# The second layer's up projection as seven block products on a fused two-layer kernel

## The chip, the cores and the metric

The kernel runs on one core of one Trainium2 chip as a single program. The metric is the device time of an execution in microseconds. The core has a matrix engine (PE, with its weight loads shown apart as PEld), a vector engine (DVE), an activation engine (ACT), Pool (GpSimd), and SP, whose queue issues the transfers here. Operands lie in SBUF; matmuls write PSUM, where the kernel has three tiles `mm` of 1024 fp32 values per partition and two tiles `ms` of 512.

## The reference

Two layers over 512 tokens of width 1024, with a context of 256 tokens in the first. The first layer's mixer is a Fourier and long-convolution block, the second's an attention with low-rank queries and keys. Behind each mixer stands the same feed-forward network, and the change lies in the second layer's:

```python
def _conv_ffn(h, w_up, conv_w, conv_b, w_down):
    gate, val = jnp.split(h @ w_up, 2, axis=-1)
    return (jax.nn.silu(_dwconv3(gate, conv_w, conv_b)) * val) @ w_down
...
        x = x + g1 * yx
        x = x + g2 * _conv_ffn(_modulate(_rms_norm(x, norm2[i]), sh2, sc2), *ffn)
```

`w_up` is 1024 x 5632 (a gate half and a value half of 2816 each), `_dwconv3` mixes three neighbouring tokens of a feature, `w_down` is 2816 x 1024. All is fp32.

## The kernel before

Every fp32 product is made of three matmuls in the rounded format fp32r. A tensor is split in a high part, which ACT rounds (`hi`, line 98), and a low part, the rest, which DVE subtracts (`lo`, line 103). `mm3` (lines 123 to 125) multiplies high by high, weights' high by tokens' low, and weights' low by tokens' high. Weights stand still in PE and tokens stream through; tokens lie transposed, features on the partitions, so a tile `hh[k]` / `hl[k]` holds 128 features of all 512 tokens.

Weights come through the pool `W`, which has three buffers each of `wr` (as loaded, by SP), `wh` and `wl`. `wload` loads 128 x 1024 values and splits them. The pool gives a new tile any buffer that is free by the order of the program.

The second layer's FFN is `ffn` (line 826). Its 2816 hidden features are 22 chunks f of 128. `up(f)` loads a gate tile and a value tile of `w_up`, runs 8 x 2 x 3 matmuls of 512 columns into two PSUM tiles, then the convolution (`conv3`, lines 322 to 324: one ACT pass and two DVE taps, all reading PSUM), Silu on ACT (line 845), the product with the value half on DVE (line 847), and the split into `ah` and `al`. Chunk 0 runs as two halves of 256 tokens, since the normalization in front of it ends in halves.

The down projection runs in three groups, chunks 0 to 7, 8 to 15 and 16 to 21. Each begins when one chunk more than the group has been emitted:

```python
        for gi, (f0, f1) in enumerate(GROUPS):
            while nxt < min(f1 + 1, NF):
                up(nxt)
                nxt += 1
```

A group is `res_proj` (line 791): eight output tiles m, each with one `w_dn` tile through `wload`, 24 matmuls of 512 columns (18 in the last group), and one DVE instruction (line 808) that adds the gated result to the residual `x[m]`. The last group does its last four m in halves of 256 tokens.

In front of the FFN stands the attention's output projection, also a `res_proj`, with the normalization's work hooked between its tiles (`norm_hook`): per feature tile and half a scaling on DVE (line 266), an ACT pass that adds the shift and rounds (267), and a DVE instruction for the low part (271).

A scheduler in the framework orders each engine's instructions from what the program emits; an engine then runs its queue strictly in that order.

Of the kernel before, what the change touches and what calls it, by code (L numbers as in the profile page):

```python
# [18 lines left out]
P = 128  # L19
D = 1024  # L20
KD = 8
T = 512
# [3 lines left out]
NF = 22  # L26
GROUPS = ((0, 8), (8, 16), (16, 22))
# [23 lines left out]
class Builder:  # L51
# [169 lines left out]
    def norm(self, i, k, x, hh, hl, c0, n, tp):  # L221


        nc = self.nc
        j = 1 if c0 >= C0 else 0
        box = {}
# [47 lines left out]
        def apply(d, step=None):  # L274
# [3 lines left out]
                ins = low(d)  # L278
            return ins

        return stat, fin, apply

    def norm_hook(self, first, second):

# [541 lines left out]
    def ffn(self, i, x, hh, hl, width, segs, first_segs, late, fill=None, hook=None, rest=None):  # L826
# [42 lines left out]
        self.close(f"ftm{i}")  # L869
        self.close(f"act{i}")  # L870

    def layer0(self):
        nc, I = self.nc, self.I
        yh, yl = self.mixer()
        nt = self.pool("nt", bufs=3)
        hp = self.pool("h2p")
        self.xp = self.pool("xres")
        tp = lambda: self.t(nt, [P, 512], F32, "nt")
        x = [self.t(self.xp, [P, TW], F32, f"xr{d}") for d in range(KD)]
# [38 lines left out]
        nhook, rest = norms(1, 0)  # L918
# [30 lines left out]
    def attention(self, x, hh, hl, rest):  # L949
        nc, I = self.nc, self.I  # L950
        v = nc.vector
        sg = ((0, 512), (512, 260))
        st = ((0, T), (C0, C))
        tok = [128 * k for k in range(4)] + [C0, C0 + 128]
        dr = self.pool("dr", space=bass.MemoryType.DRAM)
        xd = self.t(dr, [KD, P, T], F32, "xd")
# [29 lines left out]
        for a in range(2):  # L986
            r = tp()
# [213 lines left out]
        self.close("pq")  # L1201
        self.close("psB")
        self.ps = self.pool("psA", space=PSUM)
        oh, ol = [], []
        op = self.pool("op")
        for p in range(KD):
            oh.append(self.t(op, [P, T], F32R, f"oh{p}"))
            ol.append(self.t(op, [P, T], F32R, f"ol{p}"))
# [1 line left out]
            self.lo(ol[p], O[p], oh[p])  # L1210
        self.close("pO")
        self.close("pa")
        return oh, ol, xd

    def layer1(self, x, hh, hl, rest):
        nc, I = self.nc, self.I
        oh, ol, xd = self.attention(x, hh, hl, rest)
        nt = self.pool("nt", bufs=3)
        hp = self.pool("h2p")
        self.xp = self.pool("xres")  # L1220
        tp = lambda: self.t(nt, [P, 512], F32, "nt")
        x = [self.t(self.xp, [P, T], F32, f"xr{d}") for d in range(KD)]
        for d in range(KD):
            nc.sync.dma_start(x[d], xd[d])
        half = [[(0, 256)], [(256, 256)]]
        hh = [self.t(hp, [P, T], F32R, f"hh{d}") for d in range(KD)]
        hl = [self.t(hp, [P, T], F32R, f"hl{d}") for d in range(KD)]
        hook, rest = self.norm_hook(*[self.norm(1, 1, x, hh, hl, c, 256, tp) for c in (0, 256)])
        self.res_proj(1, 2, oh, ol, KD, lambda m: I["w_o"][m], x, [(0, T)], half, hook)
        rest()  # L1230
        self.dbg("xa1", x)
        self.ffn(1, x, hh, hl, T, [(0, T)], half, None)
        return x

    def build(self):
        nc = self.nc
        self.setup()
        x = self.layer1(*self.layer0())
        for d in range(KD):
            nc.sync.dma_start(self.out[d], x[d][:, 0:T])  # L1240
        for n in ("xres", "h2p", "nt", "op", "dr", "psA", "sm", "W", "P0"):
            self.close(n)


# [195 lines left out]
```

## Time and profile before

| what | value |
|---|---|
| median of 3 runs | 1831.08 us (1829.17 to 1833.47) |
| profiled execution | 1830.64 us, span 1828.8 us |
| mean granted PE clock | 0.958 |
| PE busy | 1706.3 us, 93% of the span |
| DVE busy | 1022.0 us, 56% |
| ACT busy | 613.9 us, 34% |
| Pool busy | 121.3 us, 7% |
| HBM | 94 GB/s over the span |

Lines such as L103 are lines of the kernel. A group's row tells engine, line, operation, written tile <- read tiles (buffer numbers left out), shapes and counts. A timeline row has start, duration, engine, line, operation, and in brackets how long the engine had idled and what ended that. Matmul rows are pipelined, so a matmul's cost is read from start to start and not from its duration. One part of the page gives the span in 40 slices, with the busy share in tenths and the granted PE clock, another the chain of work that ended last. The second layer's FFN lies from about 1450 us to the end.

### The profile page before, as it was taken

What the parts mean: (1) busy time and instruction counts of PE and PEld (TensorE: products, weight loads), DVE (VectorE), ACT (ScalarE), POOL (GpSimd) and SP (SyncE); (2) the same over time, 40 slices, a digit from 0 to 9 for tenths busy, and PEclk for the clock granted to TensorE, in tenths of its full rate; (3) what the DMA queues carried; (4) which work ended last, traced back from release to release, by engine and by line L of the source; (5) the groups of instructions that cost most, each with busy time, mean ns of one, the idle gap of its engine ahead of it and who ended that gap; (6) DMA issues with size and microseconds to landing.
All of it is one profiled execution on the core that took longest, in us unless ns stands there. A gap on an engine that the chain in (4) does not pass through costs nothing.

```text
span 1828.8 us, 21719 instructions
## 1 busy us (share of the span) xinstructions
PE 1706.3 (93%) x8742; PEld 1326.3 (73%) x8742; DVE 1022.0 (56%) x1662; ACT 613.9 (34%) x830; POOL 121.3 (7%) x202
## 2 busy tenths in 40 slices
PE   6889975799899999999999887899998999999999
PEld 2657864787688888888888556555554777888887
DVE  3486966864898435543434554665764554444443
ACT  3332222323323212222122434655663443223231
POOL 0052113310000000000000000110110000000000
PEclk7799987899999999999999998899999999999999
DMA  9032520352355234431312310000002323322322
GB/s 351 24 127 71 171 78 30 103 173 81 116 174 176 88 104 140 147 128 70 121 47 85 117 60 24 1 12 12 12 12 70 116 72 101 104 93 92 104 75 98
DMA packets 53249, 172.83 MB, mean 95 GB/s; under 512 B 6043, under 2 KB 8925, under 8 KB 52125
## 3 DMA queue, kind: packets, MB, share of 16 engines
q1 hardware_dynamic: 53149, 171.45, 27.4%
q8 instruction: 69, 1.13, 0.2%
q14 instruction: 31, 0.25, 0.0%
HBM read 167.23 MB, written 4.19 MB: 94 GB/s over the span
## 4 chain that ended last, share of the span: by engine, by line
PE 77%; DVE 11%; ACT 5%; POOL 3%; issue 3%; DMA 1%; POOLq 0%; SPq 0%; ACTq 0%; DVEq 0%
PE mm L123 21%; PE mm L124 20%; PE mm L125 20%; PE pv L1176 2%; PE ms L234 2%; PE z L1164 2%; DVE junk L210 2%; DVE wl L103 1%; DVE S L1154 1%; PE s L1130 1%; ACT S L1145 1%; PE s L123 1%; PE s L124 1%; PE s L125 1%; POOL s L388 1%
## 5 line engine op out<-in xcount | busy, mean ns | idle before, releaser
L123 PE MATMUL mm<-hh,wh 128*128 128x512 f32 (+2 forms) x1344 | 474.7, 356 | 7.0 <-ACT wh L98 3.4
L124 PE MATMUL mm<-hl,wh 128*128 128x512 f32 (+2 forms) x1344 | 473.9, 353 | 4.9 <-DVE hl L271 4.6
L125 PE MATMUL mm<-hh,wl 128*128 128x512 f32 (+2 forms) x1344 | 473.2, 353 | 1.3 <-DVE wl L103 1.3
L98 ACT ACTIVATE wh<-wr 128x1024 fp32r<-128x1024 f32 (+2 forms) x200 | 206.2, 1031 | 717.5 <-PE mm L124 646.5
L103 DVE TENSOR_TENSOR wl<-wr,wh 128x1024 fp32r<-128x1024 f32 (+2 forms) x200 | 243.6, 1219 | 287.3 <-ACT wh L98 279.6
L123 PEld LDWEIGHTS mm<-hh,wh 128*128 128x128 f32 x1344 | 254.4, 190 | 57.1 <-issue 12.0
L124 PEld LDWEIGHTS mm<-hl,wh 128*128 128x128 f32 x1344 | 255.0, 190 | 42.9 <-DVE hl L271 7.5
L125 PEld LDWEIGHTS mm<-hh,wl 128*128 128x128 f32 x1344 | 254.5, 190 | 38.4 <-issue 2.5
L123 PE MATMUL mm<-ah,wh 128*128 128x512 f32 (+1 forms) x528 | 187.8, 356 | 0.0
L124 PE MATMUL mm<-al,wh 128*128 128x512 f32 (+1 forms) x528 | 187.7, 356 | 0.0
L125 PE MATMUL mm<-ah,wl 128*128 128x512 f32 (+1 forms) x528 | 187.3, 355 | 0.0
L210 DVE SCALAR_TENSOR_TENSOR junk<-wr,sb 128x1024 bf16<-128x1024 f32 x128 | 159.3, 1244 | 36.7 <-DMA wr<-wmodT 36.6
L808 DVE SCALAR_TENSOR_TENSOR xr<-mm,mod,xr 128x512 f32<-128x512 f32 (+1 forms) x100 | 62.2, 642 | 204.3 <-PE mm L125 204.0
L123 PEld LDWEIGHTS mm<-ah,wh 128*128 128x128 f32 x528 | 99.1, 188 | 19.2 <-DVE xr L808 2.5
L124 PEld LDWEIGHTS mm<-al,wh 128*128 128x128 f32 x528 | 99.2, 188 | 15.3 <-issue 0.8
L125 PEld LDWEIGHTS mm<-ah,wl 128*128 128x128 f32 x528 | 99.2, 188 | 14.6
L1145 ACT ACTIVATE S<-s,rks 128x512 f32<-128x512 f32 x96 | 63.4, 688 | 44.3 <-PE s L125 43.4
L1154 DVE TENSOR_TENSOR S<-S,mb 128x1536 f32<-128x1536 f32 x32 | 54.8, 1752 | 20.7 <-POOL mb L1151 20.7
L845 ACT ACTIVATE fg<-fg 128x772 f32<-128x772 f32 (+1 forms) x44 | 32.6, 741 | 100.3 <-DVE fg L324 89.3
L1176 PE MATMUL pv<-S,V 128*64 128x512 f32 x192 | 58.9, 620 | 0.0
L1164 PE MATMUL z<-S,ones 128*32 128x512 f32 x192 | 42.7, 699 | 13.7 <-ACT S L1155 11.3
L1155 ACT ACTIVATE S<-S 128x1536 f32<-128x1536 f32 x32 | 47.1, 1481 | 18.0 <-DVE S L1154 18.0
(318 smaller groups left out, 2282.6 us busy)
## 6 DMA issues: line engine op xcount, KB each, us to landing
wr<-w_up SPq DMA_DIRECT2D x88, 512.0 KB, 3.3
wr<-wmodT SPq DMA_DIRECT2D x80, 512.0 KB, 3.3
wr<-w_dn SPq DMA_DIRECT2D x32, 512.0 KB, 3.2
wm<-wmod0a SPq DMA_DIRECT2D x8, 1024.0 KB, 9.6
wr<-w_in SPq DMA_DIRECT2D x16, 512.0 KB, 3.2
wr<-w_dn SPq DMA_DIRECT2D x20, 384.0 KB, 3.1
wr<-w_out SPq DMA_DIRECT2D x12, 512.0 KB, 3.2
wr<-w_o SPq DMA_DIRECT2D x12, 512.0 KB, 3.2
```

Source lines behind the costliest of these rows:

```text
L98: self.nc.scalar.activation(dst, src, AF.Copy)
L103: (eng or self.nc.vector).tensor_tensor(dst, src, hi.bitcast(F32), op=ALU.subtract)
L123: mmul(out, wh, xh, start=start, stop=False)
L124: mmul(out, wh, xl, start=False, stop=False)
L125: mmul(out, wl, xh, start=False, stop=stop)
L210: nc.vector.scalar_tensor_tensor(junk, raw, 1.0, self.sb[:, j, :], op0=ALU.mult, op1=ALU.mult, accum_out=acc)
L808: nc.vector.scalar_tensor_tensor(x[m][:, a2:b2], ps[:, a2:b2], mod[:, 8 * sec + m, j : j + 1], x[m][:, a2:b2], op0=ALU.mult, op1=ALU.add)
L1145: nc.scalar.activation(S[j // 3][:, j % 3, :], ps, AF.Copy, scale=rs[:, 2 * j + a : 2 * j + a + 1])
L1154: v.tensor_tensor(s, s, mb3.to_broadcast([P, 3, T]), op=ALU.subtract)
L1155: nc.scalar.activation(s, s, AF.Exp)
L1164: nc.tensor.matmul(z[32 * g : 32 * g + 32, :], self.ones32, Ss[g // 2][(2 * k + g % 2) // 3][:, (2 * k + g % 2) % 3, :], start=k == 0, sto ...
L1176: nc.tensor.matmul(pv[64 * a : 64 * a + 64, :], V[:, k, 64 * h : 64 * h + 64], Ss[a][k // 3][:, k % 3, :], start=k == 0, stop=k == 5, tile ...
```

## The change

The second layer's up projection no longer multiplies whole chunks. Split the inner 1024 into two halves, the 512 tokens into two halves, and a chunk's output into gate and value: that is a 2 x 2 by 2 x 2 block product, in which eight block products of 128 x 512 by 512 x 256 are replaced by seven, in Winograd's form of Strassen's algorithm, with sums of blocks ahead and behind. Each block product is 4 x 3 matmuls of 256 columns.

- `layer1` keeps the normalized tokens as plain fp32 (`hf`, in buffers of the later `act1` pool) and as four quarter blocks in high and low parts. `apply_f` makes them: the scaling on DVE, the shift on ACT, then a separate rounding on ACT and the low part on DVE.
- `combos`, called after chunk 0, makes four sums of token blocks: 16 Pool instructions of 256 columns, each result split by ACT and DVE into `T1` to `T4`.
- Chunks 0 and 1 go the old way (`plain`), both in halves of 256 tokens.
- For chunks 2 to 21 `weights(f)` loads both `w_up` tiles, lets Pool form four sums of 512 columns in `s13` and `s24` (one buffer each), and splits four tiles: the gate tile (through `W`), half of the value tile (`vh`, `vl`, low part on Pool), `s13` (`zh`, `zl`), and `s24` (through `W`). It is emitted one chunk ahead of `strassen(f)`.
- `strassen(f)` runs the seven products into PSUM and adds them up on DVE, with two ACT copies and two Pool adds; the gate part is put together in `G` in SBUF, from where the convolution reads it, and the value part in an SBUF tile.
- The group rule stays, so `weights(9)` and `weights(17)` are emitted ahead of the down projections of the first and second group.

```diff
+    def apply_f(self, d, src, fin, f, h, l, tp):
+        n = src.shape[-1]
+        A, B = self.A[1][1][:, 0, :], self.mod[1][:, 24:32, 0]
+        u = tp()
+        self.nc.vector.scalar_tensor_tensor(u[:, :n], src, A[:, d : d + 1], fin.box["R"][:, :n], op0=ALU.mult, op1=ALU.mult)
+        self.nc.scalar.activation(f, u[:, :n], AF.Identity, bias=B[:, d : d + 1])
+        self.hi(h, f)
+        self.lo(l, f, h)
...
+    def ffn_s(self, i, x, hf, quarter, ap, nt):
...
+        zp = self.pool("zp", bufs=2)
+        tm = self.pool("ftm", bufs=2)
...
+        def combos():
+            for k in range(4):
+                a, b = hf[k], hf[k + 4]
...
+                g.tensor_tensor(t1, a[:, H:], a[:, :H], op=ALU.subtract)
+                g.tensor_tensor(t2, b[:, H:], t1, op=ALU.subtract)
+                g.tensor_tensor(t3, b[:, H:], a[:, H:], op=ALU.subtract)
+                g.tensor_tensor(t4, t2, b[:, :H], op=ALU.subtract)
+                for n, t_ in enumerate((t1, t2, t3, t4)):
+                    self.hi(tq[n + 1, 0][:, k, :], t_)
+                    self.lo(tq[n + 1, 1][:, k, :], t_, tq[n + 1, 0][:, k, :])
...
+        def weights(f):
+            a1, a2 = (self.wraw(I["w_up"][i, f, q]) for q in range(2))
+            s13 = self.t(zp, [P, 1024], F32, "s13", 1)
+            s24 = self.t(zp, [P, 1024], F32, "s24", 1)
+            g = nc.gpsimd
+            g.tensor_tensor(s13[:, 512:], a2[:, :512], a2[:, 512:], op=ALU.add)
+            g.tensor_tensor(s13[:, :512], a1[:, :512], a2[:, :512], op=ALU.subtract)
+            g.tensor_tensor(s24[:, :512], s13[:, 512:], a1[:, :512], op=ALU.subtract)
+            g.tensor_tensor(s24[:, 512:], a1[:, 512:], s24[:, :512], op=ALU.subtract)
+            w1 = split(self.W, ("wh", "wl"), a1)
+            w22 = split(zp, ("vh", "vl"), a2[:, 512:], g)
+            w13 = split(zp, ("zh", "zl"), s13)
+            w24 = split(self.W, ("wh", "wl"), s24)
...
+        def product(f, n, dst):
+            (wh, wl), (bh, bl) = wt[f][n], blocks[n]
+            for k in range(4):
+                w = slice(128 * k, 128 * k + 128)
+                self.mm3(dst, wh[:, w], wl[:, w], bh[k], bl[k], k == 0, k == 3)
+            return dst
+
+        def strassen(f):
+            ta, tb, tc_ = (self.t(nt, [P, 512], F32, "nt") for _ in range(3))
+            p1, p5, u2, u3, c21, c22 = (t_[:, o : o + H] for t_ in (ta, tb, tc_) for o in (0, H))
+            G = self.t(tm, [P, T], F32, "G")
+            pp, g = self.mm(), nc.gpsimd
+            nc.scalar.copy(p1, product(f, 1, pp[:, 0:H]))
+            v.tensor_tensor(G[:, :H], product(f, 2, pp[:, 512 : 512 + H]), p1, op=ALU.add)
+            pp = self.mm()
+            v.tensor_tensor(u2, product(f, 6, pp[:, 0:H]), p1, op=ALU.add)
+            nc.scalar.copy(p5, product(f, 5, pp[:, 512 : 512 + H]))
+            g.tensor_tensor(p1, u2, p5, op=ALU.add)
+            pp = self.mm()
+            v.tensor_tensor(G[:, H:], product(f, 3, pp[:, 0:H]), p1, op=ALU.add)
+            v.tensor_tensor(u3, product(f, 7, pp[:, 512 : 512 + H]), u2, op=ALU.add)
+            g.tensor_tensor(c22, u3, p5, op=ALU.add)
+            gate = conv(f, G)
+            v.tensor_tensor(c21, u3, product(f, 4, self.ms()[:, :H]), op=ALU.subtract)
+            finish(f, gate, [tc_])
+
+        def up(f):
+            if f < NP:
+                plain(f)
+                if f == NP - 1:
+                    weights(NP)
+            else:
+                if f + 1 < NF:
+                    weights(f + 1)
+                strassen(f)
+
+        NP = 2
...
+            late = [[(0, H)], [(H, H)]] if gi == 2 else None
+            self.res_proj(i, 5, [acts[f][0] for f in range(f0, f1)], [acts[f][1] for f in range(f0, f1)], f1 - f0, wsrc, x, [(0, T)], late, None)
...
-        self.ffn(1, x, hh, hl, T, [(0, T)], half, None)
+        self.ffn_s(1, x, hf, quarter, ap, nt)
```

In the changed kernel the four weight sums are lines 958 to 961, the Pool adds of `strassen` lines 991 and 995, and its two DVE sums of the third PSUM tile lines 993 and 994.

More of the change, by code (lines that the diff above doesn't have):

```diff
@@ L279, in apply @@
             return ins
+        fin.box = box
         return stat, fin, apply
+    def apply_f(self, d, src, fin, f, h, l, tp):
[6 more added lines that the diff above has]
+        self.lo(l, f, h)
     def norm_hook(self, first, second):
@@ L1203, in attention, with layer1 @@
         self.ps = self.pool("psA", space=PSUM)
+        return O, xd
+    def layer1(self, x, hh, hl, rest):
+        nc, I = self.nc, self.I
+        O, xd = self.attention(x, hh, hl, rest)
+        nt = self.pool("nt", bufs=3)
+        hp = self.pool("h2p")
+        self.xp = self.pool("xres")
+        op = self.pool("op")
         oh, ol = [], []
-        op = self.pool("op")
         for p in range(KD):
@@ L1212, in attention @@
         self.close("pa")
[L1213 to L1220, printed above, removed]
         tp = lambda: self.t(nt, [P, 512], F32, "nt")
@@ L1240, in build @@
             nc.sync.dma_start(self.out[d], x[d][:, 0:T])
-        for n in ("xres", "h2p", "nt", "op", "dr", "psA", "sm", "W", "P0"):
+        for n in ("xres", "h2p", "nt", "dr", "psA", "sm", "W", "P0"):
             self.close(n)
```

83 lines of the change are left out of this document (80 added, 3 removed).

## The prediction

> **What bounds the kernel now.** I read the page first: spans, the 40 slices, the chain that ended last.
>
> ```profile
> span 1828.8 us, 21719 instructions
> PE 1706.3 (93%) x8742; PEld 1326.3 (73%) x8742; DVE 1022.0 (56%) x1662; ACT 613.9 (34%) x830; POOL 121.3 (7%) x202
> ...
> PE   6889975799899999999999887899998999999999
> ...
> POOL 0052113310000000000000000110110000000000
> PEclk7799987899999999999999998899999999999999
> ...
> PE 77%; DVE 11%; ACT 5%; POOL 3%; issue 3%; DMA 1%; POOLq 0%; SPq 0%; ACTq 0%; DVEq 0%
> ...
> wr<-w_up SPq DMA_DIRECT2D x88, 512.0 KB, 3.3
> ```
>
> TensorE is the path, and the last eight slices (the second layer's FFN) are full while Pool is empty. The busy time in stretches (columns: stretch, length, PE, PEld, DVE, ACT, POOL, clock, DMA share, GB/s) says so for some eight chunks and for one group of down projections; the other two stretches, in the attention and in the output projection, are there for their clocks.
>
> ```profile
> 1475.00:1565.00 90.00, 90.00 (x392) 72.65 (x391) 43.19 (x52) 33.59 (x42) 0.00 (x0) 1.00 0.30 98
> 1565.00:1610.00 45.00, 45.00 (x200) 37.28 (x199) 17.30 (x19) 9.64 (x10) 0.00 (x0) 1.00 0.31 109
> ...
> 1100.00:1145.00 45.00, 35.35 (x182) 27.95 (x182) 22.19 (x60) 19.71 (x29) 0.00 (x0) 0.85 0.07 24
> ...
> 1428.00:1446.00 18.00, 18.00 (x136) 15.82 (x135) 9.45 (x18) 6.47 (x9) 0.00 (x0) 1.00 0.44 147
> ```
>
> In the first two PE is busy every microsecond, DVE not half of it. One chunk f on DVE, in order of time:
>
> ```profile
> 1517.09 1.23 DVE L103 TENSOR_TENSOR wl<-wr,wh 128x1024 fp32r<-128x1024 f32 x1 [4.61 <-ACT wh L98]
> 1518.23 0.74 DVE L323 SCALAR_TENSOR_TENSOR fg<-mm,pcol,fg 128x511 f32<-128x511 f32 x1
> 1518.89 1.22 DVE L103 TENSOR_TENSOR wl<-wr,wh 128x1024 fp32r<-128x1024 f32 x1
> ...
> 1521.53 0.69 DVE L847 TENSOR_TENSOR fg<-fg,mm 128x512 f32<-128x512 f32 x1 [0.76 <-ACT fg L845]
> 1522.91 0.69 DVE L103 TENSOR_TENSOR al<-fg,ah 128x512 fp32r<-128x512 f32 x1 [0.70 <-ACT ah L98]
> 1528.19 1.23 DVE L103 TENSOR_TENSOR wl<-wr,wh 128x1024 fp32r<-128x1024 f32 x1 [4.58 <-ACT wh L98]
> ```
>
> A chunk takes 1528.19 - 1517.09 = 11.10 us for 48 matmuls of 512 columns. From start to start a 1024-wide low part costs DVE 1.14 (1518.23 - 1517.09), a convolution tap 0.66, so a 512-wide product 0.60 (the same 0.09 less than its row).
>
> **The change, part by part.**
>
> *Matmuls.* A Strassen chunk has 7 x 4 x 3 = 84 matmuls of 256 columns. The output projection before shows that width back to back, first and 34th after it:
>
> ```profile
> 1442.44 0.28 PE L123 MATMUL mm<-oh,wh 128*128 128x256 f32 x1
> ...
> 1446.51 0.28 PE L124 MATMUL mm<-ol,wh 128*128 128x256 f32 x1
> ```
>
> 4.07 / 34 = 0.1197 us, so 10.06 us a chunk, 10.3 with the 0.2 that a chunk now loses at its seams (11.10 less 48 x 0.2267, the pace of the projections below). If PE stayed the bound, 20 chunks would gain 20 x 0.8 = 16 us.
>
> *What DVE and Pool get.* Per chunk Pool forms four sums of 512 (`s13`, `s24`, lines 958 to 961 of the changed kernel), the low part of the seventh weight block (512), and two adds of 256 (lines 991, 995). DVE has three 1024-wide low parts (was two), two taps, the product, the low part of `act`, and five 256-wide sums out of PSUM. Durations, from the early stage where Pool works (Pool rows: shortest/median/longest ns):
>
> ```profile
> L388 POOL TENSOR_TENSOR s<-s,s x12: 1261/1512/2357, 95.2 to 143.9; 128x512 f32<-128x512 f32 x12
> ...
> L619 POOL TENSOR_TENSOR tm<-tm,tm x4: 726/733/1711, 213.4 to 267.3; 128x256 f32<-128x256 f32 x4
> ...
> 113.26 2.49 POOL L449 TENSOR_TENSOR s<-s,brow 128x512 f32<-128x512 f32 x2 [8.15 <-DVE s L448]
> ...
> 113.10 0.68 DVE L450 TENSOR_TENSOR s<-mm,S 128x512 f32<-128x512 f32 x1
> ...
> 97.23 1.10 DVE L103 TENSOR_TENSOR apl<-s,aph 128x512 fp32r<-128x512 f32 x1 [1.00 <-ACT aph L98]
> 98.49 1.57 DVE L103 TENSOR_TENSOR aml<-s,amh 128x512 fp32r<-128x512 f32 x1 [0.15 <-ACT amh L98]
> 99.98 2.31 DVE L210 SCALAR_TENSOR_TENSOR junk<-wr,sb 128x1024 bf16<-128x1024 f32 x1
> ...
> 99.47 1.74 POOL L388 TENSOR_TENSOR s<-s,s 128x512 f32<-128x512 f32 x1
> 101.18 3.93 POOL L394 TENSOR_TENSOR s<-s,s 128x512 f32<-128x512 f32 x2
> ```
>
> Alone a 512-wide Pool sum takes 1.25 (2.49 / 2), and 0.65 is my reading for 256 (0.73 less the same start-to-start margin). The rows from 97 to 105 us show the two engines taking turns: a 512-wide low part that takes 0.69 in the FFN takes 1.10 and 1.57, the 1024-wide one 2.31, Pool's sums 1.74 and 1.97. At 113 us, where DVE reads one operand from PSUM, neither is slower. So DVE instructions with both operands in SBUF and Pool's sums exclude each other. One turn of each took 101.18 - 99.47 = 1.71, where 1.25 + 0.60 = 1.85 would be alone.
>
> The Trainium skill, "SBUF — State Buffer", section "Who interferes with whom", states that a DVE instruction with two SBUF inputs and a GpSimd instruction that reads SBUF share one port pair, held for a whole instruction while the other engine fully blocks. By that rule no time is saved at a change of turns, a chunk would cost 14.3 instead of the 13.8 below, and the sum would be 15 x 0.5 = 7.5 us more; the trace's 1.71 against 1.85 is 8% milder.
>
> *One chunk.* Exclusive time: Pool 5 x 1.25 + 2 x 0.65 = 7.55; DVE 3 x 1.14 (low parts) + 2 x 0.66 (taps, now reading `G` from SBUF) + 2 x 0.60 (product with `tc_`, low part) = 5.94; together 13.49. Can they be hidden in one another's waits? The built program's queues say no. `s24` has one buffer, so Pool's third sum waits for DVE's low part of the last `s24`; Pool's add at line 991 stands behind the four sums; DVE's line 993 waits for that add, and the taps, `s13`'s low part and the product stand behind 993; Pool's next `s13` sum waits for that low part (`s13` has one buffer too). Each engine idles while the other makes what it needs. DVE's 993 and 994 (0.40 each, Pool waiting for them) come on top: 14.3; the turns give 0.5 back (four at 0.14): 13.8 us. Bounds: 12.3 (PSUM sums wholly hidden, more saved at turns) and 14.6. PE needs 10.06, ACT (rows below: three 1.06, four about 0.63, two of 0.4, conv 0.76) 7.3: both inside.
>
> ```profile
> 1515.99 1.06 ACT L98 ACTIVATE wh<-wr 128x1024 fp32r<-128x1024 f32 x1 [4.25 <-PE mm L124]
> 1516.96 0.76 ACT L322 ACTIVATE fg<-mm,pcol 128x512 f32<-128x512 f32 x1
> ...
> 1522.24 0.63 ACT L98 ACTIVATE ah<-fg 128x512 fp32r<-128x512 f32 x1 [0.75 <-DVE fg L847]
> ```
>
> A chunk prepares weights for the next but one. Chunks 8, 16, 20 and 21 prepare none, 9 and 17 find half done: 15 full chunks. 15 x (13.8 - 11.1) = +40.5; five at PE's pace, 5 x (10.3 - 11.1) = -4. Sum **+36.5**.
>
> *Down projections.* `weights(9)` and `weights(17)` come before the projections of their groups, and hold two of the three `wh`/`wl` buffers. In the built program all eight `w_dn` tiles of each of the first two groups lie at one address. So a high part waits until the projection before has ended, where now it runs one ahead:
>
> ```profile
> 1571.56 0.39 PE L124 MATMUL mm<-al,wh 128*128 128x512 f32 x1
> ...
> 1588.31 1.06 ACT L98 ACTIVATE wh<-wr 128x1024 fp32r<-128x1024 f32 x1 [4.38 <-PE mm L124]
> 1593.75 1.06 ACT L98 ACTIVATE wh<-wr 128x1024 fp32r<-128x1024 f32 x1 [4.38 <-PE mm L124]
> ```
>
> A projection takes 5.44 (24 x 0.2267). From the last L124's start: 0.39 to its end, 1.06 high part, 1.23 low part, some 0.15 between them: the first L125 starts at 2.83 instead of 4 x 0.2267 = 0.91. Each such seam costs 1.9 us. The first is free (its buffer comes free three products early), the second is mostly filled by chunk 9's product 4 (0.6 left), five stand bare: 9.5. At the eighth PE first meets chunk 10's product 4: its `w_up` half starts loading when projection 6's buffer is split (0.5 into it), lands 3.3 later, three Pool sums make 7.55, a turn of DVE 8.7, the low part 9.95, and PE stands there since 5.68: 4.3. So 14.4 a group, two groups **+28.8** (bounds 2 x 9.5 and 2 x 17). The third group holds nothing and rotates as now: 0.
>
> *The start.* `apply_f` adds an ACT pass to each of 16 pieces; then `combos` adds 16 Pool instructions of 256, 16 high and 16 low parts. The second half's normalization on DVE, first and last rows, and chunk 2's first tap:
>
> ```profile
> 1465.38 1.26 DVE L266 SCALAR_TENSOR_TENSOR nt<-xr,A,ms 128x256 f32<-128x256 f32 x3 [0.95 <-PE ms L256]
> ...
> 1471.16 0.89 DVE L271 SCALAR_TENSOR_TENSOR hl<-nt,mod,hh 128x256 fp32r<-128x256 f32 x2 [0.18 <-ACT hh L267]
> ...
> 1495.98 0.74 DVE L323 SCALAR_TENSOR_TENSOR fg<-mm,pcol,fg 128x511 f32<-128x511 f32 x1
> ```
>
> `combos` pairs piece k with k + 4, so it can start at about 1469, after the fifth; Pool then has 16 x 0.65 + 5 x 1.25 (`weights(3)` stands before the last four) = 16.7, and turns with about 12 us of two-operand DVE work: T4 is whole near 1498. Chunk 2's matmuls end near 1495.5 now and so begin near 1484.5; with one product ahead of it PE reaches product 4 near 1487: **+11** (bounds 3 and 16). Chunk 1 in halves: 96 x 0.1197 against 48 x 0.2267, **+0.6**. `G` added in Pool, `xd` read earlier, pools opened in another order: nothing, under the projections' matmuls; if the residual's loads were late, DVE's sum behind a projection would wait first, and PE only when three PSUM buffers are full.
>
> *Sum.* 36.5 + 28.8 + 11.6 = 76.9. The profiled execution took 1830.64 us (span 1828.8 and 1.84 around it), 0.4 under the median of 1831.08: 1907.5, rounded to **1907**.
>
> **The rivals.** (1) *Turns fall into waits.* The chain alone, without turns: low part of `s24` 1.23, two sums and an add 3.15, line 993 0.40, 1.14, 0.66, 0.40, 0.66, 0.40, 1.14, product 0.60, high part of `act` 0.63, of `s24` 1.06: 11.5 a chunk. 15 x 0.4 - 4 + 24 (seams without the turns) + 4 = +30: **1861**. For it: the quoted contention is from another stage; against: 13.5 of exclusive work can't fit in 11.5 unless handovers overlap far more than 0.14. (2) *The clock falls too.* At 1100 us PE was busy 35.35 of 45 and was granted 0.85. At 0.85 a chunk's matmuls need 11.8, still under 13.8, but 16 projections of 5.44 grow by 15 us: **1922**. Against: 1428 to 1446 us kept 1.00 through short gaps. (3) *The other side: faster.* DVE and Pool keep up, PE stays the bound, PE order fills the seams: 20 x -0.8 and +4 at the start: **1819**. It decides if the chunk distance is under 10.5 and the seams cost under 12 us together; 13.5 us of exclusive work speaks against it. (4) *The change does less than it says:* the 20 chunks all take the new path in the built program, so no chance.
>
> **How the numbers follow.** Forecast 0.58, (1) 0.18, (2) 0.17, (3) 0.05, between 0.02. Range: low end under (1), whose seams may cost 10 less, 1850; high end by the upper bounds, 15 x 3.5 - 4 + 34 + 16.6 = +99, 1930, and 1937 to take in most of (2) with a slow chunk. Faster by over 0.2% (3.7 us, about what three runs here can tell): 0.05, same 0.02, slower 0.93.
>
> **What would show it.** Distance of two chunks' `zl` low parts 13 to 14.5 us in steady state; DVE's `wl` and `zl` rows well over 1.23 on average and Pool's 512-wide ones near 1.7 to 2.2 (else rival 1); PE at seven tenths in the chunk slices; in projections 3 to 7 of the first two groups PE waiting 1.9 us for `wl` before an L125, none in the third; PE waiting near chunk 2's product 4. The prediction is wrong if chunks come every 10 to 11 us, or if the two engines' rows keep their lone durations.

## The result and the profile after

The changed kernel takes 1938.44 us in the median of five runs (1935.56 to 1940.03), the kernel before 1831.08 (1829.17 to 1833.47). The ratio is 1.058, with a 95% interval of 1.057 to 1.060: **slower by 107 us**. The forecast was 1907 us, slower; the direction came as said, the time lies 31 us higher, 1.4 us past the range's end of 1937. (Of the runs below, one execution of `dn_free` took 2400.01 us at a granted clock of 0.64; times and ratios leave it out.)

The page of the changed kernel, the lines that answer to those shown of before:

```profile
span 1933.5 us, 23944 instructions
PE 1731.7 (90%) x9582; PEld 1379.5 (71%) x9582; DVE 1137.1 (59%) x1806; ACT 675.9 (35%) x946; POOL 331.3 (17%) x358
...
PE   6889976898999999999998879999897778778889
...
POOL 0151123200000000000000001110105660573250
PEclk8899986899999999999999988999999899999999
...
PE 9%; POOL 5%; DVE 5%; issue 2%; ACT 2%; DMA 0%; POOLq 0%; DVEq 0%; ACTq 0%
```

The nines of PE at the end have become sevens and eights, and the sevens stand in slices where Pool now has fives to sevens. The chain that ended last was followed only through the last part of the span here (its shares add up to 23%), but in it Pool and DVE each hold about half as much as PE.

Busy time in stretches (columns: stretch, length, PE, PEld, DVE, ACT, POOL, clock, DMA share, GB/s), three chunks and six projections:

```profile
1557.00:1599.00 42.00, 34.90 (x264) 33.30 (x263) 31.23 (x39) 19.42 (x28) 24.19 (x17) 0.96 0.22 76
1606.50:1650.00 43.50, 36.23 (x146) 26.25 (x145) 10.71 (x11) 5.91 (x6) 1.22 (x1) 1.00 0.21 73
```

PE stands for a sixth of both. Neither DVE nor Pool is full in the first, but together they have 55 us of work in 42. The time between the first starts of PE's stages, on the profiled executions (span 1828.8 before, 1933.5 after):

| stage | before | after | more | forecast |
|---|---|---|---|---|
| up to the second layer's FFN | 1450.5 | 1452.5 | 2.0 | 0 |
| chunks 0 to 8 | 110.6 | 147.0 | 36.3 | 27.0 (start 11.6, six full chunks, one light) |
| projections, group 1 | 43.5 | 65.1, of it 4.3 products of chunks 9 and 10 | 17.3 | 14.4 |
| chunks 9 to 16 | 88.6 | 105.7, and those 4.3 | 21.4 | 16.4 |
| projections, group 2 | 43.5 | 65.1, of it 4.3 | 17.3 | 14.4 |
| chunks 17 to 21 | 55.2 | 61.3, and those 4.3 | 10.4 | 4.8 |
| projections, group 3 | 36.8 | 36.8 | 0 | 0 |
| sum | | | 104.7 | 77.0 |

One statement ahead of the prediction is wrong: in the kernel before, the last group did not do its last four projections in halves; `half` was passed for the first chunk alone. The halves are new, and the sum has no term for them.

A steady chunk on DVE, and the same on Pool:

```profile
1560.61 1.43 DVE L103 TENSOR_TENSOR zl<-s,zh 128x1024 fp32r<-128x1024 f32 x1
1561.96 1.77 DVE L920 TENSOR_TENSOR fg<-fg,nt 128x512 f32<-128x512 f32 x1
1563.97 0.42 DVE L987 TENSOR_TENSOR G<-mm,nt 128x256 f32<-128x256 f32 x1 [0.24 <-PE mm L125]
1564.43 1.01 DVE L103 TENSOR_TENSOR al<-fg,ah 128x512 fp32r<-128x512 f32 x1
...
1565.69 1.96 DVE L103 TENSOR_TENSOR wl<-s,wh 128x1024 fp32r<-128x1024 f32 x1
1571.15 0.42 DVE L993 TENSOR_TENSOR G<-mm,nt 128x256 f32<-128x256 f32 x1 [3.49 <-POOL nt L991]
1571.49 1.22 DVE L103 TENSOR_TENSOR wl<-wr,wh 128x1024 fp32r<-128x1024 f32 x1
...
1574.69 1.43 DVE L103 TENSOR_TENSOR zl<-s,zh 128x1024 fp32r<-128x1024 f32 x1
```

```profile
1560.92 2.26 POOL L103 TENSOR_TENSOR vl<-wr,vh 128x512 fp32r<-128x512 f32 x1
1563.15 1.74 POOL L958 TENSOR_TENSOR s<-wr 128x512 f32<-128x512 f32 x1
1564.85 1.73 POOL L959 TENSOR_TENSOR s<-wr,wr 128x512 f32<-128x512 f32 x1
1567.80 1.29 POOL L960 TENSOR_TENSOR s<-s,wr 128x512 f32<-128x512 f32 x1 [1.23 <-DVE wl L103]
1569.17 1.26 POOL L961 TENSOR_TENSOR s<-wr,s 128x512 f32<-128x512 f32 x1
1570.39 0.72 POOL L991 TENSOR_TENSOR nt<-nt,nt 128x256 f32<-128x256 f32 x1
```

The distance of the two `zl` rows is 14.08 us (forecast 13.8). Both parts of the argument can be seen: where both engines work (1561 to 1567 us) the product takes 1.77 instead of 0.69, a low part 1.96 instead of 1.23, Pool's sums 1.74 instead of 1.25; and each engine stands for the other, Pool before L960 for `s24`'s low part, DVE 3.49 us before L993 for the add behind Pool's four sums. PE stands behind DVE:

```profile
1556.66 0.39 PE L123 MATMUL mm<-T,zh 128*128 128x256 f32 x1 [2.67 <-DVE G L993]
```

### The profile page after: what moved, and what is told of

It reads as the page before. It is cut to its first block, busy times and chain, and to the rows that moved or that the text cites. A ratio compares the mean times of both kernels' runs of the same rounds, so it can differ in the third digit from the quotient of the medians.

```text
span 1933.5 us, 23944 instructions
## 1 busy us (share of the span) xinstructions
PE 1731.7 (90%) x9582; PEld 1379.5 (71%) x9582; DVE 1137.1 (59%) x1806; ACT 675.9 (35%) x946; POOL 331.3 (17%) x358
## 3 DMA queue, kind: packets, MB, share of 16 engines
q8 instruction: 75, 1.23, 0.3%
## 5 line engine op out<-in xcount | busy, mean ns | idle before, releaser
L98 ACT ACTIVATE wh<-wr 128x1024 fp32r<-128x1024 f32 (+1 forms) x184 | 188.4, 1025 | 651.2 <-PE mm L124 576.8
L123 PE MATMUL mm<-hh,wh 128*128 128x512 f32 (+1 forms) x976 | 334.5, 345 | 5.6 <-ACT wh L98 3.4
L103 DVE TENSOR_TENSOR wl<-wr,wh 128x1024 fp32r<-128x1024 f32 (+1 forms) x184 | 233.0, 1267 | 180.7 <-ACT wh L98 177.6
L124 PE MATMUL mm<-hl,wh 128*128 128x512 f32 (+1 forms) x976 | 334.5, 343 | 4.8 <-DVE hl L271 4.6
L125 PE MATMUL mm<-hh,wl 128*128 128x512 f32 (+1 forms) x976 | 334.1, 343 | 1.3 <-DVE wl L103 1.3
L123 PE MATMUL mm<-ah,wh 128*128 128x512 f32 (+2 forms) x568 | 198.8, 351 | 9.1 <-ACT wh L98 9.1
L125 PEld LDWEIGHTS mm<-hh,wl 128*128 128x128 f32 x976 | 185.6, 190 | 24.3 <-issue 2.1
L125 PE MATMUL mm<-ah,wl 128*128 128x512 f32 (+2 forms) x568 | 198.1, 349 | 5.4 <-DVE wl L103 5.3
L124 PE MATMUL mm<-al,wh 128*128 128x512 f32 (+2 forms) x568 | 197.7, 349 | 0.8 <-DVE al L103 0.8
L123 PEld LDWEIGHTS mm<-ah,wh 128*128 128x128 f32 x568 | 107.0, 189 | 31.4 <-ACT wh L98 13.8
L123 PE MATMUL mm<-B,wh 128*128 128x256 f32 x288 | 86.2, 300 | 9.2 <-ACT nt L986 7.3
L123 PE MATMUL mm<-T,zh 128*128 128x256 f32 x160 | 51.3, 321 | 41.2 <-DVE G L993 36.8
L124 PE MATMUL mm<-B,wh 128*128 128x256 f32 x288 | 84.2, 293 | 1.2 <-DVE B L103 1.1
L125 PE MATMUL mm<-B,wl 128*128 128x256 f32 x288 | 83.5, 291 | 0.1
```

What stands on the lines that cost most here:

```text
L98: self.nc.scalar.activation(dst, src, AF.Copy)
L103: (eng or self.nc.vector).tensor_tensor(dst, src, hi.bitcast(F32), op=ALU.subtract)
L123: mmul(out, wh, xh, start=start, stop=False)
L124: mmul(out, wh, xl, start=False, stop=False)
L125: mmul(out, wl, xh, start=False, stop=stop)
```

## The experiments

Ratios are against runs of the kernel before that were taken alongside, each with its 95% interval. The changed kernel stands at 1.058 (1.057 to 1.060).

### All sums on DVE (dve_all)

```diff
         def weights(f):
...
-            g = nc.gpsimd
+            g = v
...
         def strassen(f):
...
-            pp, g = self.mm(), nc.gpsimd
+            pp, g = self.mm(), v
```

> The four sums of weights, the low part of the seventh block and the two 256-wide adds run on DVE instead of Pool. Theory (two-operand DVE work and Pool sums exclude each other, 13.5 us a chunk): Pool's 7.55 us become 4 x 0.60 + 0.60 + 2 x 0.33 = 3.7 on DVE, DVE's own queue is then 5.94 + 2.0 + 3.7 = 11.6 a chunk, the chunk distance falls from 14.07 to 11.6 to 12.4: 15 x -2.1 = -31, with some 6 at the start and near the eighth projection: 1901 us (1888 to 1912), and the wl rows go back to 1.23. Rival (no turns; the DVE queue is the long chain, and Pool's sums run beside it): 3.7 us more on it, chunks of 15 to 17.7, 1955 to 1990.

1876.91 us, ratio 1.025 (1.023 to 1.027). DVE has more to do, and the kernel is 60 us faster; the time lies 24 us under the forecast and outside its range. The low parts of three chunks:

```profile
1537.40 1.22 DVE L103 TENSOR_TENSOR zl<-s,zh 128x1024 fp32r<-128x1024 f32 x1
...
1549.56 1.21 DVE L103 TENSOR_TENSOR zl<-s,zh 128x1024 fp32r<-128x1024 f32 x1
...
1561.07 1.22 DVE L103 TENSOR_TENSOR zl<-s,zh 128x1024 fp32r<-128x1024 f32 x1
```

23.67 / 2 = 11.83 us a chunk, in the range given, and the rows are back at 1.22; DVE is busy in 22.98 of these 23.67 us. The rival (15 us or more) falls. The gain is larger than the 15 x 2.24 = 34 us of the steady chunks: the first two distances after the start (24.3 and 22.0 us in the changed kernel, 21.8 and 11.3 here) give 9 us more than the steady gain, the three behind each of the first two groups (23.8, 13.8, 15.0 against 16.9, 12.3, 11.3) some 5.5 each. Pool's sums cost there too, and the forecast of this run had put no more than some 6 us there.

### Pool as busy, but reading nothing (pool_memset)

```diff
-            g.tensor_tensor(s13[:, 512:], a2[:, :512], a2[:, 512:], op=ALU.add)
-            g.tensor_tensor(s13[:, :512], a1[:, :512], a2[:, :512], op=ALU.subtract)
-            g.tensor_tensor(s24[:, :512], s13[:, 512:], a1[:, :512], op=ALU.subtract)
-            g.tensor_tensor(s24[:, 512:], a1[:, 512:], s24[:, :512], op=ALU.subtract)
+            for s in (s13[:, 512:], s13[:, :512], s24[:, :512], s24[:, 512:]):
+                for r in range(3):
+                    g.memset(s, 0.01 + 0.01 * r)
```

> Pool's four sums of weights are left out (the seven products then use constants in place of the sums), and in the place of each stand three memsets of the same 512 columns, so that Pool is busy for about as long, at the same places of its queue, with the same waits on s13 and s24, but reads nothing. Turns theory (it is the exclusion of reads that costs, not Pool's time): DVE's and Pool's rows go back to their lone durations (wl 1.23) and the chunk falls to between 10.5 and 11.8: 15 x -2.9 = -43, the start and the eighth projections some 5 better: 1890 us (1875 to 1908). Rival (Pool's 7.5 us of work and the waits between the queues make the chunk, whatever it reads): chunk of 13.3 or more, 1925 us or more, if three memsets take 1.2 or more.

1883.60 us, ratio 1.030 (1.028 to 1.031). One steady chunk of Pool and the rows of DVE beside it:

```profile
1558.06 2.28 POOL L103 TENSOR_TENSOR vl<-wr,vh 128x512 fp32r<-128x512 f32 x1
1560.27 2.87 POOL L960 MEMSET s<- 128x512 f32 x6
1563.81 0.99 POOL L960 MEMSET s<- 128x512 f32 x2 [0.67 <-DVE wl L103]
1564.85 0.74 POOL L990 TENSOR_TENSOR nt<-nt,nt 128x256 f32<-128x256 f32 x1
1565.53 1.93 POOL L960 MEMSET s<- 128x512 f32 x4
```

```profile
1557.75 1.43 DVE L103 TENSOR_TENSOR zl<-s,zh 128x1024 fp32r<-128x1024 f32 x1
1559.10 1.77 DVE L920 TENSOR_TENSOR fg<-fg,nt 128x512 f32<-128x512 f32 x1
...
1561.58 0.69 DVE L103 TENSOR_TENSOR al<-fg,ah 128x512 fp32r<-128x512 f32 x1 [0.29 <-ACT ah L98]
...
1562.53 1.23 DVE L103 TENSOR_TENSOR wl<-s,wh 128x1024 fp32r<-128x1024 f32 x1
1565.63 0.42 DVE L992 TENSOR_TENSOR G<-mm,nt 128x256 f32<-128x256 f32 x1 [1.87 <-POOL nt L990]
...
1569.18 1.43 DVE L103 TENSOR_TENSOR zl<-s,zh 128x1024 fp32r<-128x1024 f32 x1
```

Twelve memsets take 5.79 us, more than the 5.0 of the four sums alone; the order of Pool's queue and its waits on `s13` and `s24` stand as they were. Yet the chunk falls from 14.08 to 1569.18 - 1557.75 = 11.43 us. Beside memsets `al` takes 0.69 and `wl` 1.23; beside `vl`, which still reads, the product still takes 1.77. So 2.65 us a chunk are the turns of these four sums, and they belong to Pool's reads, not to its time. What is left, 11.43, is near what the first rival had given for the chain of waits alone (11.5), and 0.3 us over the chunk of before. That this chain is now the limit is read from the rows and not tested: DVE stands 1.87 us a chunk for Pool's add at line 990, neither of the two engines is full (18.5 and 19.7 us of work in the 22.9 of two chunks), and one turn, the product's against `vl`, is still in it. Two things go with the sums here besides: the memsets do not wait for the loads, and the low parts of `s13` for the first two Strassen chunks come 60 and 79 us earlier, which helps the start and so the time, but not the steady chunk.

The section of the Trainium skill cited in the prediction ("SBUF — State Buffer", "Who interferes with whom") also states that such a DVE instruction contends with a Pool instruction that reads SBUF and not with one that only writes it. The two lone durations beside memsets agree.

### Two buffers for the sums (two_s)

```diff
-            s13 = self.t(zp, [P, 1024], F32, "s13", 1)
-            s24 = self.t(zp, [P, 1024], F32, "s24", 1)
+            s13 = self.t(zp, [P, 1024], F32, "s13", 2)
+            s24 = self.t(zp, [P, 1024], F32, "s24", 2)
...
-        ap = self.pool("act1", bufs=10, side="right")
+        ap = self.pool("act1", bufs=9, side="right")
```

> s13 and s24 get two buffers each (the act1 pool gives up one of its ten slots for the room), so Pool's sums no longer wait for DVE's low parts of the last ones. Turns theory: 13.49 us of work that excludes itself stays, only the 0.6 us a chunk in which both waited goes: chunk distance 13.2 to 13.8, 15 x -0.5 = -8, 1930 us (1920 to 1936). Rival (the single buffers tie Pool and DVE into one chain, and this chain sets the pace): the chunk falls to 11 or less, 15 x -3 = -45, 1893 us (1880 to 1905).

1941.69 us, ratio 1.061 (1.059 to 1.064): nothing gained. Steady chunks:

```profile
1558.57 1.44 DVE L103 TENSOR_TENSOR zl<-s,zh 128x1024 fp32r<-128x1024 f32 x1
1572.39 1.43 DVE L103 TENSOR_TENSOR zl<-s,zh 128x1024 fp32r<-128x1024 f32 x1
1586.21 1.43 DVE L103 TENSOR_TENSOR zl<-s,zh 128x1024 fp32r<-128x1024 f32 x1
```

13.82 us, 0.3 over the 13.49 of work that excludes itself, in the first group; in the second the distances are 12.4 to 15.1. The rival (11 or less) falls: with this link of the chain cut, the turns keep the pace. The 8 us expected were lost elsewhere: Pool runs a chunk further ahead, so three more sums stand before the add that chunk 9 waits for, and the first distance behind each of the first two groups grows from 23.8 to 28.7 us.

### Two adds left on Pool (dve_sums)

As `dve_all`, but the adds of `strassen` stay on Pool.

> As the run with all sums on DVE, but the two 256-wide adds of the products stay on Pool (0.65 alone each). Turns theory: DVE's queue is 0.66 shorter (about 11.0) but is blocked for most of Pool's 1.3: chunk 11.6 to 12.3, within 8 us of that run: 1877 us (1869 to 1885). Rival (no turns): the adds are free on Pool, chunk 11.0 to 11.2, 1863 us.

1882.55 us, ratio 1.029 (1.027 to 1.030). Chunks come alternately 13.35 and 10.82 us apart, 12.08 in the mean against 11.83 with these adds on DVE. Even 1.3 us of Pool cost more than 0.66 on a DVE that is the bound; that they were free is refuted.

### The weights of chunks 9 and 17 behind the projections (dn_free)

```diff
-                if f + 1 < NF:
+                if f + 1 < NF and f + 1 not in (9, 17):
                     weights(f + 1)
...
+            if gi < 2:
+                weights(f1 + 1)
```

> Only the place of weights(9) and weights(17) changes: they are emitted behind the down projections of their groups instead of ahead of them, so the projections find three rotating wh/wl buffers. Theory (held buffers make the seams): the projections of the first two groups go back from 7.58 us apart to 5.44, and the wait near chunk 10's product 4 goes; each group's stage falls from 65.1 to 43.5 us, and 4.3 us of chunk 9's and 10's products move back behind it: 2 x -17.3 = -35, so 1904 us (1895 to 1915). Rival (the seams come from DVE and Pool taking turns over the weights of the next chunk, not from the buffers): the projections stay over 7 us apart, less than 10 us gained, above 1928.

1904.09 us, ratio 1.041 (1.039 to 1.042); 1904 had been expected. The rows are those of one more execution of the same kernel, of 1901.75 us:

> The kernel with weights(9) and weights(17) behind the projections once more, for its rows at the full clock: projections 5.44 us apart in the first two groups, the chunk distance still 14, span 1900.

DVE's sums behind five projections of the first group, of the changed kernel and of this one:

```profile
1612.82 0.75 DVE L819 SCALAR_TENSOR_TENSOR xr<-mm,mod,xr 128x512 f32<-128x512 f32 x1 [5.50 <-PE mm L125]
...
1650.69 0.75 DVE L819 SCALAR_TENSOR_TENSOR xr<-mm,mod,xr 128x512 f32<-128x512 f32 x1 [5.50 <-PE mm L125]
1664.77 0.75 DVE L819 SCALAR_TENSOR_TENSOR xr<-mm,mod,xr 128x512 f32<-128x512 f32 x1 [8.91 <-PE mm L125]
```

```profile
1597.81 0.75 DVE L819 SCALAR_TENSOR_TENSOR xr<-mm,mod,xr 128x512 f32<-128x512 f32 x1 [1.31 <-PE mm L125]
...
1620.21 0.75 DVE L819 SCALAR_TENSOR_TENSOR xr<-mm,mod,xr 128x512 f32<-128x512 f32 x1 [3.52 <-PE mm L125]
```

The first lie (1650.69 - 1612.82) / 5 = 7.57 apart and end with 14.08; the second 22.40 / 4 = 5.60. The seams are the held buffers'. But 5.60 isn't 5.44: here the expectation was wrong, and the last group of experiments is about it. Nor did the chunks stay at 14: on this execution three of them behind the first group came 15.4 us apart, and chunks 9 to 16 took 114.2 us against the 110.0 of the changed kernel. So the time came out as said partly by luck: the two projection stages took 44.8 us each and not 43.5, and the start and the time before the FFN were 7.4 us shorter here; why the chunks grew longer is open.

### Two more plain chunks (np4)

```diff
-        NP = 2
+        NP = 4
```

> Four plain chunks instead of two ahead of the first Strassen chunk, so that the sums of tokens have 23 us more. Theory (T4 is late for chunk 2, and the loss at the start is this wait): the two plain chunks cost 11.5 each where chunks 2 and 3 now lie 24 and 22 us apart; up to the first projection 126 us instead of 147: 1918 us (1912 to 1926), no wait of PE for T,vl at the first Strassen chunk. Rival (the first Strassen chunks are slow by themselves, wherever they stand): only two chunks of 14.07 turned into 11.5, 1933 us.

1921.11 us, ratio 1.051 (1.048 to 1.053). Of the wait for the sums of tokens, 8.04 us in the changed kernel,

```profile
1502.75 0.58 PE L123 MATMUL ms<-T,vh 128*128 128x256 f32 x1 [8.04 <-ACT T L98]
```

nothing is left; the theory holds. The stage up to the first projection took 133.5 us and not 126, on an execution of 1928.32 us, 7 above the median: PE still stood idle for 3.1 and 3.4 us, until 1498 and 1534 us.

### The halves undone (late_none)

```diff
-            late = [[(0, H)], [(H, H)]] if gi == 2 else None
+            late = None
```

> The last group's last four projections go back to whole tiles of 512 tokens, as in the kernel before; four fewer loads of w_dn and half as many residual sums. Both theories put this part of the change at nothing: 1938 us, within 3. Were it not free, the last four tiles would be faster by the seams of four more tiles, up to 8 us: 1930.

1935.97 us, ratio 1.058 (1.056 to 1.060): the part that the prediction had missed costs nothing that can be measured.

### Three edits together, and fewer Strassen chunks (best, mix_alt, mix_two)

`best` has `dve_all`, `dn_free` and `np4`.

> All three edits together: the sums on DVE, weights(9) and weights(17) behind the projections, four plain chunks. If the terms add up: 1877 - 34 (seams) - 9 (start, with chunks of 11.8 a plain one costs no more than a Strassen one) = 1834 us (1828 to 1850), about the kernel before; it cannot be much faster, since a chunk of 11.8 on DVE stands against 11.1 before. Rival (one loss takes the place of another, for one the late weights of chunks 9 and 17 behind DVE's longer queue): above 1855.

1838.80 us, ratio 1.005 (1.003 to 1.007). The terms, with the start counted at 9 us beside `dve_all`, add up to within 5 us, and all but some 10 of the 107 us are gone with the three causes. (Each edit alone had gained 61.5, 34.4 and 17.3 us, 113 together: at the start and around the projections two of them mend the same loss.) It is still slower than before: the last steady chunks of the second group come 12.1 us apart, against 11.1.

Then Strassen only where DVE has time. The token blocks lie 512 wide again, so that plain chunks can run as before:

```diff
+        def plain(f):
+            ws = [self.wload(I["w_up"][i, f, q]) for q in range(2)]
+            if f + 1 in S:
+                weights(f + 1)
...
+            if f not in S:
+                plain(f)
+            else:
+                if f + 1 in S:
+                    weights(f + 1)
+                strassen(f)
+        S = (4, 6, 11, 13, 15, 18, 20)
```

In `mix_two` the set is (4, 5, 7, 10, 11, 13, 14, 18, 19, 21). All their sums are on DVE.

> Strassen chunks stand between plain ones: 4, 6, 11, 13, 15, 18 and 20 by Strassen with all sums on DVE, the other 15 plain and 512 columns wide again, chunks 8, 9, 16 and 17 plain, so that no weights are held through the projections. Theory (the loss was DVE's and Pool's work per chunk, the held buffers and the late sums of tokens, and nothing else): a pair needs 11.6 + 4.8 = 16.4 of DVE in 10.3 + 11.1 = 21.4 of PE, so PE is the bound again and each of 7 Strassen chunks gives 0.8: 1829 - 6 = 1823 us (1819 to 1829). Rival (each change between the two kinds of chunk costs PE a microsecond, for the weights through three buffers): 14 changes, 1837 us.

> The same with ten Strassen chunks, four of the pairs behind one another (4, 5, 7, 10, 11, 13, 14, 18, 19, 21). Theory: two Strassen chunks and a plain one need 28 us of DVE in 31.7 of PE, PE stays the bound: 1829 - 8 = 1821 us (1815 to 1830). Rival (DVE comes too late where two stand together, as its work is not spread): 1.5 us lost at each of the four pairs, 1827, or with the loss at changes 1840.

1829.76 us, ratio 1.0017 (1.0005 to 1.0028), and 1834.83 us, ratio 1.0032 (1.0022 to 1.0042). Neither number came. With seven Strassen chunks the rival's loss at changes (1837) is not there in full; with ten the time lies between the rival's two numbers, 1827 and 1840, so a loss where two stand together isn't ruled out. Of the 6 to 8 us of gain the times show nothing.

### The place of the operands in SBUF (act_steps, after_pad, mix_pad, mix_pad_t)

In the traces of the changed kernels so far the projections' 512-wide matmuls come every 0.2333 us in the mean, and in the kernel before every 0.2267, at a granted clock of 1.00 in both; 24 of them make 5.60 and 5.44. In `mix_alt` even within one chunk the twelve matmuls on the token blocks `B0` took 0.2333 each, and of the twelve on `B1` the last six 0.2267. By the layout of the built programs, `B0` and `act` start 992 bytes over a multiple of 1024, `B1` and before's `act` and `hh` 544; the traces hold no addresses. In `act_steps`, made from `mix_alt`, each tile of `act` is 32 bytes longer:

```diff
-            ah, al = [self.t(ap, [P, T], F32R, q) for q in ("ah", "al")]
+            ah, al = [self.t(ap, [P, T + 8], F32R, q)[:, :T] for q in ("ah", "al")]
```

> In the changed kernel a 512-wide matmul of the projections comes every 0.2333 us, in the kernel before every 0.2267; in the run with alternate plain chunks the same holds chunk-wise between the token blocks at one place of SBUF (start address 992 bytes over a multiple of 1024) and at the other (544 over). Here each tile of act is 32 bytes longer, so the tiles start at every 32nd byte from 448 to 960 over a multiple of 1024, all else as in that run. Theory (the start address sets the pace): the pace changes by tile, 0.2267 at some and 0.2333 at other offsets, in a pattern; at offset 544 it is 0.2267. Rival (the right end of SBUF is slower as such, or the pace is that of the stage): 0.2333 at all offsets.

The mean over the three matmuls of one pair `ah[k]`, `al[k]`, worked out from the starts of PE's rows, now differs from pair to pair, from 0.228 to 0.234 in the first two groups, where it had been 0.2333 for all. So the pace changes with the place; but no pair came at 0.2267, and a rule that gives the pace from the offset doesn't come out of these rows. (The time, 1828.77 us in one run against 1829.00 for the kernel before in one, tells nothing.) Three kernels then move tiles by 448 bytes:

```diff
+        pad = self.pool("pad", side="right")
+        self.t(pad, [P, 112], F32, "pad")
         ap = self.pool("act1", bufs=10, side="right")
...
         tpool = self.pool("tq")
+        self.t(tpool, [P, 112], F32, "padt")
```

The first edit makes `after_pad` from the changed kernel and, put ahead of `B0`'s pool, `mix_pad` from `mix_alt`; `mix_pad_t` has both.

> The changed kernel with 448 empty bytes per partition ahead of act1, so that the tiles ah and al start 544 bytes over a multiple of 1024, as in the kernel before, and not 992; nothing else. Theory (the place sets the pace of the projections' matmuls, and 0.16 us of each seam of 2.14 is this pace): projections of the first two groups 7.42 us apart instead of 7.58, 512-wide ones of the third 4.08 instead of 4.20; the halves of 256 slower, 2.16 instead of 2.04; in all 3 us less, 1935 us. Rival (the pace belongs to the stage or the code, not the place): rows unchanged, 1938 us.

> The run with alternate plain chunks, and the same 448 bytes ahead of the right-hand pools, so that ah, al and the token blocks B0 start at offset 544. Theory: 24 matmuls in each of 14 plain chunks and 24 in each of 20 whole projections gain 0.0067 us each, 2.3 + 3.2 = 5.5 us: 1824 us (1821 to 1827), faster than the kernel before by 0.1 to 0.4%. Rival: 1830 us as without.

> As the last one, with 448 bytes more ahead of the sums of tokens T, so that these 256-wide operands start at offset 992, where halves of act took 0.1133 us and not 0.1197. Theory (the pace of 256-wide matmuls hangs on the place too, the other way round): 48 matmuls in each of 7 Strassen chunks gain 0.0064 each: 2.1 us, 1822 us. Rival (the halves of act were faster for another reason): 1824 us as the run before, T rows at 0.1197.

| kernel | us | ratio | 512-wide | halves of `act`, 256 | `T`, 256 |
|---|---|---|---|---|---|
| after_pad | 1939.80 | 1.060 (1.058 to 1.061) | 0.2267 | 0.1200 | 0.120 |
| mix_pad | 1827.15 | 0.9990 (0.9981 to 0.9999) | 0.2267 | 0.1200 | 0.119 to 0.120 |
| mix_pad_t | 1828.27 | 0.9995 (0.9985 to 1.0005) | 0.2267 | 0.1200 | 0.117 to 0.119 |

Projections of `mix_alt`, then of `mix_pad`:

```profile
1567.98 0.75 DVE L819 SCALAR_TENSOR_TENSOR xr<-mm,mod,xr 128x512 f32<-128x512 f32 x1 [3.52 <-PE mm L125]
1573.58 0.75 DVE L819 SCALAR_TENSOR_TENSOR xr<-mm,mod,xr 128x512 f32<-128x512 f32 x1 [3.52 <-PE mm L125]
```

```profile
1569.49 0.75 DVE L819 SCALAR_TENSOR_TENSOR xr<-mm,mod,xr 128x512 f32<-128x512 f32 x1 [3.35 <-PE mm L125]
1574.93 0.75 DVE L819 SCALAR_TENSOR_TENSOR xr<-mm,mod,xr 128x512 f32<-128x512 f32 x1 [3.35 <-PE mm L125]
```

5.60 has become 5.44, at the right end of SBUF as before, so that end isn't slow as such. In `after_pad` the projections come 7.47 apart instead of 7.57 (7.42 had been expected), and its halves go from 0.1133 to 0.1200, as said. Its sum of 3 us can't be found in the median. `mix_pad` gained 2.6 us by the medians and 4.9 by the ratios, of 5.5 expected; it is the only kernel here whose interval lies under 1, by 0.1% and just so; that is no more than a tie. On the third run the theory fell: at offset 992 the `T` operands come at 0.117 to 0.119 by product and not at 0.1133, so one offset does not decide for 256-wide operands; why the halves of `act` ran at 0.1133 stays open.

PE's stages in `mix_pad` show what became of the saving. Chunks 9 to 16 took 85.9 us against 88.6 before (three Strassen chunks, 2.4 expected) and chunks 17 to 21 53.7 against 55.2 (two, 1.6): there the 0.8 us a chunk is had. But chunks 0 to 8, with two more Strassen chunks, took 112.4 against 110.6. So on this one execution the loss lies ahead of the first projections, where the tokens are also prepared for the block products; no run tells which part of that work makes it.

## Why the prediction was right in kind and too low

- **Full chunks, 13.8 us: right.** Measured 14.08 in the steady state, 0.27 more, and 13.8 in the mean of all thirteen full chunks behind chunk 2, by the distances of line 997, a chunk's last sum; that the mean meets the forecast so well is partly luck, since single distances run from 11.4 to 16.2. The exclusion is shown by taking away the reads (11.43) or Pool's part (11.83), the sum of 13.49 by cutting a link of the chain (13.82). Rival 1 falls with the rows, which did not keep their lone durations. Without the start-to-start gain at turns, 0.5 us a chunk, the forecast was 14.3, and 14.08 lies between the two. By the Trainium skill's rule that the prediction cites ("SBUF — State Buffer", "Who interferes with whom") there is no such gain; the trace stands about halfway.
- **The held buffers, 2 x 14.4: right, too small by 5.8.** Measured 2 x 17.3: six distances of 7.57 and one of 14.08. Over 5.60 that is 6 x 1.97 less the 1.44 of chunk 9's product, 10.4 us (predicted 10.1), and 8.48 less the 2.88 of two products, 5.6 (predicted 4.3); the slower matmuls add 192 x 0.0067 = 1.3.
- **Light and half-done chunks: the step that failed.** The sum put chunks that prepare nothing at PE's pace, 10.3 us, and let 9 and 17 "find half done", 12.05 us each. By the distances of line 997 chunk 16 took 11.5 us and chunk 20 12.3; only chunk 21, with 9.1, was as light as that. And being half done relieved chunks 9 and 17 of nothing: with two of its seven products (2.9 us) already made among the projections, chunk 9 still ended 12.8 us after PE had left them at 1664.57, 15.7 in all, and chunk 17 likewise. Chunks 11 and 12 then came 15.0 us behind the ones before, which chunk 13 with 11.4 made good. That sum of chunks 9 to 12:

```profile
1677.37 0.41 DVE L997 TENSOR_TENSOR nt<-nt,ms 128x256 f32<-128x256 f32 x1
...
1689.73 0.41 DVE L997 TENSOR_TENSOR nt<-nt,ms 128x256 f32<-128x256 f32 x1
...
1704.74 0.41 DVE L997 TENSOR_TENSOR nt<-nt,ms 128x256 f32<-128x256 f32 x1
...
1719.72 0.42 DVE L997 TENSOR_TENSOR nt<-nt,ms 128x256 f32<-128x256 f32 x1
```

  Chunks 9 to 21 are 10.6 us of the miss (21.4 + 10.4 against 16.4 + 4.8), of which chunks 9 and 17 make 7.3 and 16, 20 and 21 some 2. Pool had started chunk 10's sums at 1660.33, before the group ended, but its third sum waited for the low part of chunk 9's `s24`, which came only behind the last projection:

```profile
1668.60 1.29 POOL L960 TENSOR_TENSOR s<-s,wr 128x512 f32<-128x512 f32 x1 [4.49 <-DVE wl L103]
```
- **The start, +11.6: right in kind, too small.** Chunks 0 to 8 cost 9.3 us more than forecast, 7.9 of it up to the end of chunk 2. Within product 4 of chunk 2 PE stood 8.0 us until 1502.75 for the next rounded piece of a sum of tokens. The prediction had the last of these sums whole near 1498; its last low part ended at 1504.90:

```profile
1504.47 0.43 DVE L103 TENSOR_TENSOR T<-fg,T 128x256 fp32r<-128x256 f32 x1 [0.20 <-ACT T L98]
```

  PE also stood 3.55 us until 1470.61 for the second half's normalization, where the kernel before stood 1.22 and then 1.19, and chunk 3 lost 3.4 us until 1529.67; neither wait had been forecast. The upper bound for the start, 16, was nearer.
- **The clock: rival 2 did not come.** 1.00 in the projections, 0.96 in the chunks, where PE has time to spare.
- **What was missing:** the halves (nothing), the place of `act` (2.6 us of the 5.8 above, by the rows), and the time before the FFN (2.0 us on one profiled execution; in the other profiled executions but that of `dn_free` PE began the FFN anywhere from 1443.5 to 1458.1, so these 2.0 us can't be called an effect of the change). The median stands 2.7 us further from before's than the spans do.

So the miss of 30 us is made of light and half-done chunks with what lies between them (10.6), the start (9.3), the held buffers (5.8), and 4.7 that no term of the change covers. The range's upper end added the upper bounds of chunks, groups and start, but held light and half-done chunks at their best case; with the 10.6 us it would have held.

## What to carry to other kernels

A sum that an idle Pool forms is not free where DVE's instructions have both operands in SBUF: add up the two engines' exclusive time per pass, and compare that, not each engine's share, with the bound. The saving of an algorithm with fewer products is small (0.8 of 11.1 us here), so count its sums first; even on the better engine they made a chunk of 11.8, and only between plain chunks, where DVE has time, did the 0.8 show. And buffers that are taken ahead of a stage which rotates through the same pool cost that stage its rotation in every step.

## What was not expected of the hardware

The same 512-wide matmul at the same granted clock takes 0.2267 or 0.2333 us by the place of its moving operand along the partition, and halves of such a tile the other way round (0.1200 and 0.1133 at the starts 544 and 992 bytes over a multiple of 1024, by the layout of the built programs). Moving tiles by 448 bytes, with nothing else changed, turned 5.60 us a projection into 5.44. A 512-wide memset on Pool takes 0.48 us, and two of DVE's two-operand instructions, of 0.69 and 1.23 us, kept their lone durations beside it.
